# Products of 128 rows in a chunked RWKV-7 recurrence, Gram products of a head pair in one go, and joins of the inverse in another PSUM pool

## The chip, the cores and the metric

The kernel runs on one core of a Trainium2 chip. The metric is device time in microseconds, the median of several runs; one further execution is recorded by the hardware profiler. A core has TensorE (PE, with its weight loads PEld), VectorE (DVE), ScalarE (ACT), GpSimd (POOL) and SyncE (SP, which issues DMAs). They run side by side, each in its own order of instructions, and wait for one another through semaphores.

## The reference

A model of 1024 tokens of width 1024 has two blocks of layers. The first mixes an RWKV-7 recurrence in both directions with MLA attention and is followed by a mixture of experts; the second (windowed attention, a gated linear recurrence, two mixtures of experts) isn't touched here. What matters is the recurrence, eight heads of 64:

```python
def step(state, inp):
    r_t, w_t, k_t, v_t, a_t, b_t = inp
    sa = einsum('bhvk,bhk->bhv', state, a_t)
    state = (state * w_t[:, :, None, :] + sa[..., None] * b_t[:, :, None, :]
             + v_t[..., None] * k_t[:, :, None, :])
    return state, einsum('bhvk,bhk->bhv', state, r_t)

zf = token_shift_centred(z, mu_prev, mu_next)      # r, k, v, wd, ad, gd
a = sigmoid(a0 + einsum('bsdr,drc->bsdc', ad, a_up))   # and decay from tanh(wd) @ w_up
y = wkv7_scan(forward) + flip(wkv7_scan(backward))
```

## The kernel before

A scheduler fixes each engine's order when the program is built; tiles come from pools with a set number of buffers, and an instruction waits until its operands are there and its buffer is free. From 37 to 629 us PE computes the projections z (lines 286 to 288: three fp32r products of high and low parts). Between them stand the preparations of the recurrence. From 631 to 1248 us attention follows: L818, L845, L856 and L873 build keys, values and queries, then come the scores S, the transposes of the probabilities (L900) and the products with the values (L914, L922). After the last finishes of the recurrence the output projection of both branches (br) starts, and from about 1340 us on nothing belongs to the change.

The recurrence works by chunks of 64 tokens: 16 chunks, two directions, four pairs of heads p. The heads of a pair lie on rows 0 to 63 and 64 to 127.

- `prep` runs for each pair, direction d and half of the tokens g (eight chunks). The lora (L580) takes two products of 512 columns, each from 64 rows of a tile. `gram` (L552) multiplies B and K, which stand block-diagonally in tiles bd of 128x128, with AR: the masked results are LT (L557), LA (L559), MB and MK. `flip` transposes (L530) and copies (L532). `put` writes all to rw in DRAM, which holds nine blocks of 128 columns for each two chunks.
- `inverse` inverts the unit triangular matrices of a pair: 32x32 blocks by substitution on DVE (L655, L657), then the two joins of each half of the tokens by products (L679, L683) in PSUM tiles pw.
- `rwkv_chain` carries the state through the 16 chunks of one pair, both directions u at once. Each step loads its blocks (rwt), and `mm` (L742) issues products of 64x64, one per head, direction and summand, that add up in PSUM: px from `ahead` (LA·VT and AN·XT, copied at L761), U = XT·px0 + px1·S (copied at L779), the next state S = KT·VT + BT·U plus the decayed SW (L775, L788), and Y = S·R + VT·MK + U·MB (L792).
- `finish` (L693 to L719) normalises the results of a pair.

Chain 0 starts at 431 us, between the projections; chain 3 ends at 1247 us. PSUM tiles pw (two buffers) belong to the preparations, pc (two buffers) to the chain.

Of the kernel before, what the change touches and what calls it, by code (L numbers as in the profile page):

```python
# [12 lines left out]
OP = mybir.AluOpType  # L13
# [181 lines left out]
class Prog:  # L195
# [22 lines left out]
    def keep(self, keep, dram):  # L218
# [7 lines left out]
        self.rw = [dram.tile([8, 128, 2, 1152], F32, name=f"rw{p}") for p in range(4)]  # L226
# [216 lines left out]

class Rwkv:
# [14 lines left out]
    def own(self, dram, pool, psw):  # L459
# [5 lines left out]
        self.L = [dram.tile([4, 128, NH, CH], F32, name=f"rL{i}") for i in range(2)]  # L465
        self.E = [dram.tile([128, 2, 32, 32], F32, name=f"rE{i}") for i in range(2)]
        for b in range(5):
# [9 lines left out]
    def t(self, name, tag="t"):  # L477
        n = {"t": 9, "l": 2}[tag]
        return (self.big if tag == "t" else self.pp).tile([128, HT], F32, name=name, tag=tag, bufs=n)
# [9 lines left out]
    def put(self, p, d, g, m, t):  # L489
        self.P.nc.sync.dma_start(self.P.rw[p][4 * g:4 * g + 4, :, d, 128 * m:128 * m + 128].rearrange("g p t -> p g t"),  # L490
                                 t.rearrange("p (g c) t -> p g (c t)", c=2))
# [34 lines left out]
    def flip(self, p, d, g, m, x):  # L526

        P, nc, ps = self.P, self.P.nc, self.ps(0)
        for q in range(4):
            nc.tensor.transpose(ps[:, 128 * q:128 * q + 128], x[:, 128 * q:128 * q + 128], P.c("ident"))  # L530
        t = self.t("flip")
        nc.scalar.activation(t, ps, AF.Copy)  # L532
        for c in range(2):
            o = 128 * m + 64 * c
            nc.sync.dma_start(P.rw[p][4 * g:4 * g + 4, :, d, o:o + 64].rearrange("g (h t) k -> t (g h) k", h=2),
                              t[64 * c:64 * c + 64].rearrange("t (x k) -> t x k", k=64))

    def diag(self, i, f):

        t = self.bd[i]  # L540
        for h in range(2):
            s = slice(64 * h, 64 * h + 64)
            f(t[s, :, s], s)
        return t

    def gram(self, lb, AR, da, mask, dr):

        P, nc = self.P, self.P.nc
        for g in range(2):
            ps = self.ps(0)  # L550
            for c in range(4):
                nc.tensor.matmul(ps[:, 128 * c:128 * c + 128], lb[:, 4 * g + c], AR[:, :, 4 * g + c], start=True, stop=True)  # L552
            v = ps.rearrange("p (c x t) -> p c x t", x=2, t=CH)
            cs = slice(4 * g, 4 * g + 4)
            m = lambda name: P.c(name)[:, None, :].to_broadcast([128, 4, CH])
            if mask is None:
                nc.scalar.activation(da[:, cs], v[:, :, 0], AF.Copy)  # L557
            else:
                nc.vector.tensor_mul(da[:, cs], v[:, :, 0], m(mask))  # L559
            nc.vector.tensor_mul(dr[:, cs], v[:, :, 1], m("m_inc"))  # L560

    def prep(self, p, d, g):
# [16 lines left out]
        for x, act in enumerate((P.twd, P.ad)):  # L579
            nc.tensor.matmul(pm[x], up[rows[x], x], act[rows[x], ts], start=True, stop=True)  # L580
# [26 lines left out]
        self.put(p, d, g, 1, AR[:, 1])  # L607
        ta3, kd3, iW3 = c3(ta), c3(kd), c3(iW)
        B = self.diag(0, lambda o, s: nc.vector.tensor_mul(o, ta3[s], iW3[s]))
        K = self.diag(1, lambda o, s: nc.vector.tensor_mul(o, kd3[s], iW3[s]))  # L610
# [9 lines left out]
        LT, MB = self.t3("rLT", "l"), self.t3("rMB")  # L620
        self.gram(B, AR, LT, None, MB)
        self.put(p, d, g, 3, MB)
        self.flip(p, d, g, 0, AR[:, 0].rearrange("p c t -> p (c t)"))
        self.flip(p, d, g, 5, ta)
        LA, MK = self.t3("rLA"), self.t3("rMK")
# [1420 lines left out]
```

## Time and profile before

| | |
|---|---|
| median of 3 runs | 4181.69 us (4176.91 to 4192.26) |
| the profiled execution | 4153.57 us |
| its span; granted clock of PE | 4151.8 us; 0.948 |
| PE busy in the span | 3737.5 us (90%) |
| DVE, ACT, POOL busy | 2816.6 (68%), 2112.2 (51%), 417.2 us (10%) |

Busy time of PE is modelled and overlaps from one matmul to the next; the distance of two starts tells what a matmul takes of PE's time. An f32 matmul leaves two records. The granted clock is a share of full speed: 1.0 is 2.4 GHz and 0.5 is 1.2 GHz, and a value between is a mean over time at either.

### The profile page before, as it was taken

What the parts mean: (1) busy time and instruction counts of PE and PEld (TensorE: products, weight loads), DVE (VectorE), ACT (ScalarE), POOL (GpSimd) and SP (SyncE); (2) the same over time, 40 slices, a digit from 0 to 9 for tenths busy, and PEclk for the clock granted to TensorE, in tenths of its full rate; (3) what the DMA queues carried; (4) which work ended last, traced back from release to release, by engine and by line L of the source; (5) the groups of instructions that cost most, each with busy time, mean ns of one, the idle gap of its engine ahead of it and who ended that gap; (6) DMA issues with size and microseconds to landing.
All of it is one profiled execution on the core that took longest, in us unless ns stands there. A gap on an engine that the chain in (4) does not pass through costs nothing. (4 is left out here: it accounts for less than half of the span.)

```text
span 4151.8 us, 57961 instructions
## 1 busy us (share of the span) xinstructions
PE 3737.5 (90%) x22538; PEld 2975.9 (72%) x22538; DVE 2816.6 (68%) x4374; ACT 2112.2 (51%) x2621; POOL 417.2 (10%) x313
## 2 busy tenths in 40 slices
PE   7999998999997979996999869999969986999994
PEld 6877776777675766664889757887748875788873
DVE  5556374958756556654366778888867766788887
ACT  4322323443332335554255546777738753677774
POOL 0000000100000014330000011111010000111101
PEclk9999998999998989998999989999979997999997
DMA  3355757563437569984233569999731355999994
GB/s 109 130 165 148 215 166 212 148 191 116 161 109 261 183 241 319 315 272 139 112 97 97 217 261 344 384 383 380 284 127 71 114 191 216 333 379 375 383 372 159
DMA packets 371044, 921.87 MB, mean 222 GB/s; under 512 B 156304, under 2 KB 214416, under 8 KB 298832
## 3 DMA queue, kind: packets, MB, share of 16 engines
q1 hardware_dynamic: 352336, 867.78, 57.9%
q0 software_dynamic: 18432, 50.36, 4.8%
q8 instruction: 178, 2.92, 0.3%
q14 instruction: 98, 0.80, 0.1%
HBM read 767.54 MB, written 167.25 MB: 225 GB/s over the span
## 5 line engine op out<-in xcount | busy, mean ns | idle before, releaser
L255 DVE TENSOR_TENSOR wlo<-wraw,whi 128x2048 fp32r<-128x2048 f32 x498 | 1134.1, 2289 | 297.9 <-ACT whi L255 295.3
L255 ACT ACTIVATE whi<-wraw 128x2048 fp32r<-128x2048 f32 x498 | 955.1, 1919 | 366.8 <-PE g L288 243.0
L287 PE MATMUL g<-wlo,xth 128*128 128x512 f32 x1280 | 509.2, 398 | 5.7 <-DVE wlo L255 5.6
L286 PE MATMUL g<-whi,xth 128*128 128x512 f32 x1280 | 511.4, 400 | 3.2 <-ACT xth L255 2.4
L288 PE MATMUL g<-whi,xtl 128*128 128x512 f32 x1280 | 506.8, 396 | 5.9 <-DVE xtl L255 5.6
L288 PEld LDWEIGHTS g<-whi,xtl 128*128 128x128 f32 x1280 | 242.6, 190 | 62.0 <-DVE xtl L255 10.6
L287 PEld LDWEIGHTS g<-wlo,xth 128*128 128x128 f32 x1280 | 243.1, 190 | 59.4 <-DVE wlo L255 7.9
L286 PEld LDWEIGHTS g<-whi,xth 128*128 128x128 f32 x1280 | 243.2, 190 | 57.3 <-ACT xth L255 4.8
L286 PE MATMUL z<-hT_hi,w_hi 128*128 128x512 f32 x592 | 240.8, 407 | 8.0 <-DVE z_out L402 6.4
L1646 POOL DMA_INDIRECT e_xg<-xm,e_ix x32 | 75.5, 2359 | 1711.2 <-DVE e_ix L1644 952.3
L287 PE MATMUL z<-hT_lo,w_hi 128*128 128x512 f32 x592 | 239.5, 404 | 0.0
L288 PE MATMUL z<-hT_hi,w_lo 128*128 128x512 f32 x592 | 238.3, 403 | 0.0
L287 PE MATMUL g<-wlo,e_hh 128*128 128x512 f32 x512 | 202.4, 398 | 15.2 <-DVE wlo L255 15.2
L286 PE MATMUL g<-whi,e_hh 128*128 128x512 f32 x512 | 204.4, 400 | 8.2 <-ACT e_hh L255 8.0
L288 PE MATMUL g<-whi,e_hl 128*128 128x512 f32 x512 | 196.5, 391 | 0.2
L775 POOL TENSOR_SCALAR SW<-S,wc 128x64 f32<-128x64 f32 x120 | 67.2, 575 | 773.6 <-DVE S L788 440.3
L286 PEld LDWEIGHTS z<-hT_hi,w_hi 128*128 128x128 f32 x592 | 113.3, 191 | 38.5 <-DVE z_out L402 6.6
L288 PEld LDWEIGHTS z<-hT_hi,w_lo 128*128 128x128 f32 x592 | 112.8, 191 | 31.6 <-issue 6.1
L287 PEld LDWEIGHTS z<-hT_lo,w_hi 128*128 128x128 f32 x592 | 113.5, 192 | 27.5 <-issue 2.3
L1246 PE MATMUL g<-wraw,m_hT 128*128 128x512 f32 x256 | 117.3, 598 | 13.6 <-ACT m_y L1247 6.8
L287 PEld LDWEIGHTS g<-wlo,e_hh 128*128 128x128 f32 x512 | 96.4, 188 | 42.9 <-DVE wlo L255 24.9
L286 PEld LDWEIGHTS g<-whi,e_hh 128*128 128x128 f32 x512 | 96.3, 188 | 32.9 <-ACT e_hh L255 14.4
(522 smaller groups left out, 8040.9 us busy)
## 6 DMA issues: line engine op xcount, KB each, us to landing
wraw<-in_w_gu SPq DMA_DIRECT2D x256, 1024.0 KB
wraw<-in_w_dn SPq DMA_DIRECT2D x128, 1024.0 KB
wraw<-in_w SPq DMA_DIRECT2D x96, 1024.0 KB
rwt<-rw SPq DMA_DIRECT2D x32, 1152.0 KB
w_raw<-in_w_in SPq DMA_DIRECT2D x37, 512.0 KB
rw<-flip SPq DMA_DIRECT2D x128, 128.0 KB
gt<-z_out SPq DMA_DIRECT2D x16, 512.0 KB
gate<-gt SPq DMA_DIRECT2D x32, 256.0 KB
```

The source lines that it names most:

```text
L255: return self.nc.scalar.activation(hi, src, AF.Copy), self.nc.vector.tensor_sub(lo, src, hi.bitcast(F32))
L286: t.matmul(ps, lh, rh, start=first, stop=False)
L287: t.matmul(ps, lh, rl, start=False, stop=False)
L288: t.matmul(ps, ll, rh, start=False, stop=last)
L775: nc.gpsimd.tensor_scalar(SW[:, d], S[:, d], P.wc[:, c, 4 * d + p:4 * d + p + 1], None, op0=OP.mult)
L1246: nc.tensor.matmul(ps, ht[:, k], w[:, k, n], start=(k == 0), stop=(k == 1))
L1646: nc.gpsimd.indirect_dma_start(out=xg, out_offset=None, in_=self.x, in_offset=bass.IndirectOffsetOnAxis(ap=ix[:, :1], axis=0))
```

## The change

In the chain the operands of two summands that are added lie one above the other on 128 rows, so that one product of 128 rows and 64 columns takes the place of two products of 64 rows. For this the state S and px share a tile SP (S of a head on its own half of the rows, px on the other), U is written into the loaded tile beside V, and rw has a new layout (one chunk, 768 columns). U, S and px are therefore copied half by half. In the preparations B and K of a head stand side by side in KB on that head's 64 rows, and `gram` multiplies them for both heads, by halves of the rows, in two PSUM tiles at once. The lora is split into quarters of 128 columns that alternate between the two tiles. The joins of the inverse take a PSUM tile pc instead of pw. The loads rwt go by two DMAs for each chunk and have three buffers instead of two.

```diff
+VU1, XX0, AN, RR, LL, W3, W2, VU0, XX1, RW = 0, 64, 128, 192, 256, 384, 512, 640, 704, 768
+VU, XX = (VU0, VU1), (XX0, XX1)
+HALF = (slice(0, 64), slice(64, 128))
...
+    def pairs(self, p, d, g, half, o, t):
+        w = t.shape[2]
         for c in range(2):
+            self.P.nc.sync.dma_start(self.P.rw[p][NH * g + c:NH * g + NH:2, HALF[half], d, o:o + w]
+                                     .rearrange("q t k -> t q k"), t[HALF[c]])
...
+    def gram(self, p, d, g, KB, AR):
         P, nc = self.P, self.P.nc
+        m = lambda name: P.c(name)[:, None, :].to_broadcast([128, 4, CH])
+        for q in range(2):
+            pm = [self.ps(0) for h in range(2)]
             for c in range(4):
+                for h in range(2):
+                    nc.tensor.matmul(pm[h][:, 128 * c:128 * c + 128],
+                                     KB[HALF[h], 4 * q + c].rearrange("p x t -> p (x t)"),
+                                     AR[HALF[h], :, 4 * q + c], start=True, stop=True)
+            lw = self.pp.tile([128, 4, 4, CH], F32, name="rLW", bufs=2)
+            for h in range(2):
+                v = pm[h].rearrange("p (c x t) -> p c x t", x=2, t=CH)
+                nc.vector.tensor_mul(lw[:, :, h], v[:, :, 0], m("m_str"))
+                nc.vector.tensor_mul(lw[:, :, 2 + h], v[:, :, 1], m("m_inc"))
+            self.put(p, d, NH * g + 4 * q, slice(0, 128), LL, lw.rearrange("p c x t -> p c (x t)"))
...
-        for x, act in enumerate((P.twd, P.ad)):
-            nc.tensor.matmul(pm[x], up[rows[x], x], act[rows[x], ts], start=True, stop=True)
+        for q in range(4):
+            for x, act in enumerate((P.twd, P.ad)):
+                o = ts.start + 128 * q
+                nc.tensor.matmul(pm[x][:, 128 * q:128 * q + 128], up[rows[x], x], act[rows[x], o:o + 128],
+                                 start=True, stop=True)
...
+            nc.vector.tensor_mul(KB[s, :, h], kd3[s], iW3[s])
+            nc.vector.tensor_mul(KB[s, :, 1 - h], ta3[s], iW3[s])
...
+        tt = [t4(self.t("flip")) for x in range(2)]
+        for x, y in enumerate((kd, ta)):
+            ps = self.flip(y)
+            for h in range(2):
+                copy(tt[h ^ x][:, :, h], ps[:, :, h])
+        for h in range(2):
+            self.pairs(p, d, g, h, W2, tt[h].rearrange("p q h k -> p q (h k)"))
+        t = t4(self.t("flip"))
+        copy(t, self.flip(v))
+        for h in range(2):
+            self.pairs(p, d, g, h, VU[h], t[:, :, h])
...
-            ps = self.ps(0).rearrange("p (x c t) -> p x c t", x=2, t=32)
+            ps = self.ps().rearrange("p (x c t) -> p x c t", x=2, t=32)
...
-                self.put(p, d, g, 8, self.inv[2 * g + d])
+                for h in range(2):
+                    self.put(p, d, NH * g, HALF[1 - h], XX[h], self.inv[2 * g + d][HALF[h]])
...
+        for l, r, half, o in terms:
+            i = nc.tensor.matmul(ps[HALF[half], o:o + 64], l, r, start=last[half] is None, stop=True,
+                                 skip_group_check=True)
+            if last[half] is not None:
+                P.order(i, last[half])
+            last[half] = i
...
+    def part(c):
+        R = pool.tile([128, 2, RW], F32, name="rwt", bufs=3)
+        for h, o in enumerate((AN, 0)):
+            nc.sync.dma_start(R[HALF[h], :, o:o + RW - AN], P.rw[p][c][HALF[h], :, o:o + RW - AN])
...
+        t = [(la[h][HALF[h], u], vu[h][HALF[h], u], 1 - h, 64 * u) for u in U2 for h in range(2)]
+        if c:
+            t += [(an[HALF[1 - h], u], xx[h][HALF[1 - h], u], h, 128 + 64 * u) for u in U2 for h in range(2)]
+        mm(ps, t)
+        for h in range(2):
+            nc.scalar.activation(SP[HALF[1 - h], :, h], v(ps)[HALF[1 - h]], AF.Copy)
+            if c:
+                nc.scalar.activation(xx[h][HALF[h]], v(ps, 128)[HALF[h]], AF.Copy)
...
+                nc.gpsimd.tensor_mul(SW[s], SP[s, :, h], P.wc[s, c, p:8:4][:, :, None].to_broadcast([64, 2, CH]))
...
+        mm(ps, [(xx[h][both[h], u], SP[both[h], u, h], 1 - h, 64 * u) for u in U2 for h in range(2)])
+        nc.vector.tensor_copy(vu[0][HALF[1]], v(ps)[HALF[1]])
+        nc.vector.tensor_copy(vu[1][HALF[0]], v(ps)[HALF[0]])
...
+            mm(ps, [(w2[h][:, u], vu[h][:, u], h, 64 * u) for u in U2 for h in range(2)])
+            SPn = new()
+            for h in range(2):
+                s = HALF[h]
+                if c:
+                    nc.vector.tensor_add(SPn[s, :, h], v(ps)[s], SW[s])
+                else:
+                    nc.vector.tensor_copy(SPn[s, :, h], v(ps)[s])
...
+        t = [(SP[HALF[h], u, h], rr[HALF[h], u], h, 64 * u) for u in U2 for h in range(2)] if c else []
+        mm(ps, t + [(vu[h][:, u], w3[h][:, u], h, 64 * u) for u in U2 for h in range(2)])
...
```

The rows that follow are PE's order as the two programs fix it: line, operation, out<-in, size, and how many in a row.

PE where attention starts, before: L742 is the chain, L818 and L845 attention, L683 a join, L552 a Gram, L580 the lora.

```order
L818 MATMUL pj<-cst,srs 128x128 x4
L742 MATMUL pc<-px,rwt 64x64 x4
L742 MATMUL pc<-S,px 64x64 x4
L742 MATMUL pc<-rwt,S 64x64 x4
L742 MATMUL pc<-rwt 64x64 x4
L818 MATMUL pj<-cst,srs 128x128 x4
L742 MATMUL pc<-rwt,U 64x64 x4
L742 MATMUL pc<-rwt 64x64 x4
L818 MATMUL pj<-cst,srs 128x128 x4
L742 MATMUL pc<-px,rwt 64x64 x4
L742 MATMUL pc<-rwt 64x64 x4
L845 MATMUL pj<-zk,wk 128x512 x2
```

The same place after (the chain is L759, attention L844, the lora L585, a Gram L555, the transposes L536, joins L700 and L704):

```order
L844 MATMUL pj<-cst,srs 128x128 x4
L585 MATMUL pw<-ad,lora_up 128x128 x4
L759 MATMUL pc<-SP,rwt 64x64 x4
L759 MATMUL pc<-rwt 64x64 x4
L759 MATMUL pc<-rwt,SP 64x64 x4
L759 MATMUL pc<-rwt 64x64 x12
L759 MATMUL pc<-SP,rwt 64x64 x4
L759 MATMUL pc<-rwt 64x64 x4
L759 MATMUL pc<-rwt,SP 64x64 x4
L759 MATMUL pc<-rwt 64x64 x12
L759 MATMUL pc<-SP,rwt 64x64 x4
L759 MATMUL pc<-rwt 64x64 x4
```

The size is that of the result, so products of 64 and of 128 rows read alike. Steps of the chain now follow one another (the shown pattern goes on until the fourth ends), with joins and Grams behind them; before, pieces of attention and of preparations stood between the products of a step.

PE among the projections, before: a Gram is one row of eight matmuls on full tiles.

```order
L287 MATMUL z<-hT_lo,w_hi 128x512
L288 MATMUL z<-hT_hi,w_lo 128x512
L286 MATMUL z<-hT_hi,w_hi 128x512
L552 MATMUL pw<-rAR,bd_199 128x128 x8
L287 MATMUL z<-hT_lo,w_hi 128x512
L288 MATMUL z<-hT_hi,w_lo 128x512
```

After, by the numbers of the tiles: the halves of a Gram write pw_1420 and pw_1421.

```order
L288 MATMUL z_5191<-hT_hi_212,w_lo_5161 128x512
L408 MATMUL z_5219<-cstb_67,z_pad_5157 128x2 x4
L555 MATMUL pw_1420<-rAR_1384,rKB_1392 128x128 x4
L555 MATMUL pw_1421<-rAR_1384,rKB_1392 128x128 x4
L408 MATMUL z_5219<-cstb_67,z_pad_5157 128x2 x4
L286 MATMUL z_5237<-hT_hi_212,w_hi_5233 128x512
```

The two halves stand four and four, each on 64 rows, and other work follows them.

PE at the end of attention, before: L914 and L922 are attention, L742 the chain, L695 and L497 the finishes, br the output projection.

```order
L742 MATMUL pc<-px,rwt 64x64 x4
L742 MATMUL pc<-S,px 64x64 x4
L742 MATMUL pc<-rwt,S 64x64 x4
L742 MATMUL pc<-rwt 64x64 x4
L900 MATMUL pt<-cst,p 128x128 x4
L914 MATMUL po<-pts,V 64x128 x8
L742 MATMUL pc<-rwt,U 64x64 x4
L914 MATMUL po<-pts,V 64x128 x7
L922 MATMUL po<-cst,m 64x128 x2
L695 MATMUL pc<-y_8353,cstb 128x512
L497 MATMUL pc<-cstb,t_8362 128x2 x4
L286 MATMUL br_12610<-oh,whi 128x512
```

After (L926, L940 and L948 are attention's):

```order
L948 MATMUL po<-cst,m 64x128 x2
L926 MATMUL pt<-cst,p 128x128 x4
L940 MATMUL po<-pts,V 64x128
L926 MATMUL pt<-cst,p 128x128 x8
L940 MATMUL po<-pts,V 64x128 x15
L948 MATMUL po<-cst,m 64x128 x2
L286 MATMUL br_12328<-oh,whi 128x512
L287 MATMUL br_12328<-ol,whi 128x512
```

Chain and finishes now stand ahead of these rows, and the output projection follows attention directly.

## Rows read from the trace of the kernel before

**Rows 1.** Windows: busy us of each engine (instructions), then PEclk, DMA share, GB/s.

```profile
37.00:1250.00 1213.00, 1144.25 (x9921) 886.93 (x9920) 746.28 (x1663) 410.42 (x777) 70.58 (x126) 0.96 0.52 155
630.00:712.00 82.00, 65.10 (x671) 48.34 (x670) 44.51 (x87) 27.24 (x58) 7.29 (x12) 0.77 0.76 228
1250.00:1275.00 25.00, 13.48 (x40) 9.56 (x41) 16.06 (x34) 10.12 (x11) 0.00 (x0) 0.59 0.95 350
```

**Rows 2.** Timeline of PE: start us, duration us, instruction, x records, at two places.

```profile
430.51 0.40 PE L286 MATMUL z<-hT_hi,w_hi 128*128 128x512 f32 x1
430.75 0.40 PE L287 MATMUL z<-hT_lo,w_hi 128*128 128x512 f32 x1
431.07 0.45 PE L742 MATMUL pc<-rwt 64*64 64x64 f32 x8
431.45 0.50 PE L288 MATMUL z<-hT_hi,w_lo 128*128 128x512 f32 x1
...
549.04 0.40 PE L288 MATMUL z<-hT_hi,w_lo 128*128 128x512 f32 x1
549.37 0.45 PE L742 MATMUL pc<-px,rwt 64*64 64x64 f32 x8
...
550.22 0.50 PE L286 MATMUL z<-hT_hi,w_hi 128*128 128x512 f32 x1
```

**Rows 3.** Waits of PE, 37 to 1250 us: total us, times, longest us.

```profile
PE pc L742 <- DVE S L788: 5.1, 3, 2.6
PE pc L742 <- ACT px L761: 4.7, 4, 3.3
...
PE pc L742 <- DMA rwt<-rw: 3.4, 1, 3.4
PE pc L742 <- DVE U L779: 3.2, 5, 1.1
```

**Rows 4.** Timeline of PE: products with attention's values, column halves.

```profile
1245.39 1.09 PE L914 MATMUL po<-pts,V 128*64 128x128 f32 x16
1246.41 0.45 PE L742 MATMUL pc<-rwt,U 64*64 64x64 f32 x8
```

**Rows 5.** Timeline of PE: a Gram, full tiles.

```profile
192.31 1.95 PE L552 MATMUL pw<-rAR,bd 128*128 128x128 f32 x16
194.01 0.48 PE L287 MATMUL z<-hT_lo,w_hi 128*128 128x512 f32 x1
```

**Rows 6.** Timeline of PE: the lora, one half alone and both halves.

```profile
216.84 1.12 PE L580 MATMUL pw<-twd,lora_up 64*128 64x512 f32 x2
217.89 0.49 PE L288 MATMUL z<-hT_hi,w_lo 128*128 128x512 f32 x1
...
251.82 0.69 PE L580 MATMUL pw<-twd,lora_up 64*128 64x512 f32 x1
251.83 0.69 PE L580 MATMUL pw<-ad,lora_up 64*128 64x512 f32 x1
...
252.88 0.50 PE L286 MATMUL z<-hT_hi,w_hi 128*128 128x512 f32 x1
```

**Rows 7.** Groups by line, 37 to 1250 us: busy us, mean ns | idle before.

```profile
L761 ACT ACTIVATE px<-pc 128x256 f32<-128x256 f32 (+1 forms) x64 | 24.0, 376 | 69.0 <-PE pc L742 68.9
...
L779 DVE COPY U<-pc 128x128 f32<-128x128 f32 x64 | 18.2, 285 | 37.3 <-PE pc L742 36.9
...
L792 ACT ACTIVATE Y<-pc 128x128 f32<-128x128 f32 x64 | 17.5, 274 | 60.6 <-PE pc L742 60.4
...
L788 DVE TENSOR_TENSOR S<-pc,SW 128x128 f32<-128x128 f32 x56 | 16.0, 285 | 27.3 <-PE pc L742 26.9
```

**Rows 8.** Timeline of PE, then of ACT, at the end of attention.

```profile
1247.61 0.48 PE L922 MATMUL po<-cst,m 128*64 128x128 f32 x3
...
1264.13 0.79 PE L286 MATMUL br<-oh,whi 128*128 128x512 f32 x1 [2.58 <-ACT whi L255]
...
1258.48 0.63 ACT L255 ACTIVATE oh<-oraw 128x512 fp32r<-128x512 f32 x1 [10.07 <-DMA oraw<-om]
```

More of the change, by code (lines that the diff above doesn't have):

```diff
@@ L225, in keep @@
         self.gt = [dram.tile([128, T], F32, name=f"gt{j}") for j in range(16)]
-        self.rw = [dram.tile([8, 128, 2, 1152], F32, name=f"rw{p}") for p in range(4)]
+        self.rw = [dram.tile([NCH, 128, 2, RW], F32, name=f"rw{p}") for p in range(4)]
         self.kn = [dram.tile([128, T], F32, name=f"kn{j}") for j in range(4)]
@@ L464, in own @@
             self.P.nc.gpsimd.memset(t, 0.0)
-        self.L = [dram.tile([4, 128, NH, CH], F32, name=f"rL{i}") for i in range(2)]
         self.E = [dram.tile([128, 2, 32, 32], F32, name=f"rE{i}") for i in range(2)]
-        for b in range(5):
+        for b in range(3):
             t = pool.tile([128, NH, 128], F32, name=f"bd{b}", bufs=1)
@@ L477, in t @@
     def t(self, name, tag="t"):
[L478 to L479 removed]
+        return self.big.tile([128, HT], F32, name=name, tag=tag, bufs=9)
     def t3(self, name, tag="t"):
@@ L551, in gram @@
             for c in range(4):
[L552 to L559, printed above, removed]
@@ L728, in rwkv_chain @@
     U2 = range(2)
-    h2 = [slice(0, 64), slice(64, 128)]
     pst = lambda: psum.tile([128, 512], F32, name="pc", bufs=2)
-    new = lambda name: pool.tile([128, 2, CH], F32, name=name, bufs=2)
-    v = lambda ps: ps[:, 0:128].rearrange("p (u t) -> p u t", t=CH)
+    v = lambda ps, o=0: ps[:, o:o + 128].rearrange("p (u t) -> p u t", t=CH)
     def mm(ps, terms):
         last = [None, None]
-        n = len(terms(0))
-        for x in range(n):
-            for u in U2:
-                l, r, o = terms(u)[x]
-                for h in range(2):
-                    i = nc.tensor.matmul(ps[h2[h], 128 * o + 64 * u:128 * o + 64 * u + 64], l[h2[h]], r[h2[h]],
-                                         start=(x == 0 and u == 0), stop=(x == n - 1), skip_group_check=True)
-                    if last[h] is not None:
-                        P.order(i, last[h])
-                    last[h] = i
@@ L748, in parts @@
-    def parts(c):
-        if c % 2 == 0:
-            parts.R = pool.tile([128, 2, 1152], F32, name="rwt", bufs=2)
-            nc.sync.dma_start(parts.R, P.rw[p][c // 2])
-        o = CH * (c % 2)
-        return [parts.R[:, :, 128 * m + o:128 * m + o + CH] for m in range(9)]
-    def ahead(c, q):
-        AN, _, LA, _, _, _, _, VT, XT = q
-        n = 2 if c else 1
-        ps = pst()
-        mm(ps, lambda u: [(LA[:, u], VT[:, u], 0)] + ([(AN[:, u], XT[:, u], 1)] if c else []))
-        t = pool.tile([128, 2, 2, CH], F32, name="px", bufs=2)
-        nc.scalar.activation(t[:, 0:n], ps[:, 0:128 * n].rearrange("p (x u t) -> p x u t", u=2, t=CH), AF.Copy)
-        return t
@@ L764, in rwkv_chain @@
-    S = None
-    q = parts(0)
-    px = ahead(0, q)
+        for l, r, half, o in terms:
[8 more added lines that the diff above has]
+            nc.sync.dma_start(R[HALF[h], :, o:o + RW - AN], P.rw[p][c][HALF[h], :, o:o + RW - AN])
+        one = lambda m: R[:, :, m:m + CH]
+        two = lambda *m: [one(x) for x in m]
+        return (one(AN), one(RR), two(LL, LL + CH), two(W2, W2 + CH), two(W3, W3 + CH), two(*VU), two(*XX))
@@ L767, in rwkv_chain @@
+    new = lambda: pool.tile([128, 2, 2, CH], F32, name="SP", bufs=3)
+    q, SP = part(0), new()
+    ahead(0, q, SP)
     for c in range(NCH):
-        _, Rr, _, MB, MK, BT, KT, VT, XT = q
+        _, rr, _, w2, w3, vu, xx = q
         if c % 2 == 0:
@@ L795, in rwkv_chain @@
                 nc.sync.dma_start(P.yd[4 * d + p][:, CH * (c - 1):CH * (c + 1)], Y[:, d].rearrange("p c t -> p (c t)"))
-        S = Sn
         if c < NCH - 1:
-            q = parts(c + 1)
-            px = ahead(c + 1, q)
+            q = part(c + 1)
+            ahead(c + 1, q, SPn)
+        SP = SPn
 def mla(P, dram, pool, psum):
```

94 lines of the change are left out of this document (36 added, 58 removed).

## The prediction

> **What bounds the kernel now.** I first read the windows view of the stage that the change touches [rows 1]. From 37 to 1250 us PE is busy 1144.25 of 1213 us at a granted clock of 0.96, DVE 746.28, ACT 410.42, POOL 70.58. So this stage is bound by PE, with two soft places: 630 to 712, where attention starts (65.10 of 82 us, granted clock 0.77), and 1250 to 1275 (13.48 of 25, clock 0.59). After 1340 us both kernels issue the same work, and I count nothing there.
>
> In a stage bound by PE a change is worth the time between starts of PE's instructions, not their modelled durations, which overlap. So I read starts from the timeline. The recurrence's small products stand between projection matmuls that start every 0.24 us (430.51, 430.75). Eight records of L742 (an f32 matmul leaves two) push the next projection matmul from 0.24 to 0.70 us after the last; twenty-four push it to 1.18 [rows 2]. Sixteen records more cost 0.48 us: **29 to 30 ns a record** (I use 29.2). The rest, 0.70 − 0.235 − 8 × 0.0292 = 0.23 us, belongs to the block itself: it goes from full tiles to 64x64 tiles and back, **0.12 us for each change of tile shape**.
>
> Then the waits. In this stage PE waited on the recurrence's U 3.2 us, on its px 4.7, on its state S 5.1, together 12 times [rows 3]. The hand-offs between engines are nearly all hidden by preparations, projections and attention.
>
> **The change part by part.**
>
> *Stacked summands in the chain.* Over four chains the program issues 2224 matmuls of 64x64 before, and after it 1488: 736 fewer. Of those left about half have 128 rows and 64 columns. The question is what such a one costs. Before, the two heads of a pair sit on different rows and columns of the array, and 29.2 ns is the price of two running side by side. The stacked form fills all rows, so its two halves can run side by side only by columns. The trace has that form in L914, 128*64 tiles with twice the moving columns: 16 records in 1245.39 to 1246.41, less the 0.09 that a shape change costs in these starts, 58 ns a record [rows 4]. A full-tile matmul of 128 columns takes 1.70 us for 16 records, 106 ns each [rows 5]. 58 is near half of 106, so column halves do overlap, and 64 columns should cost half of 58, 29 ns. Term: 736 × 2 × 29.2 ns = **−43 us**. Other bound: 0, if with 64 columns the halves don't overlap (then the 736 × 2 records left in stacked form cost twice 29.2 ns, which gives back what the fewer ones save).
>
> *Joint Grams.* Before, 256 matmuls of block-diagonal 128 rows at 2 × 106 ns: 54 us. After, 256 matmuls that use 64 rows each. Row halves overlap fully where one of each half is next to another: in the lora both halves took 251.82 to 252.88, 1.06 us, and one half alone took 216.84 to 217.89, 1.05 us [rows 6]. All paired, that saves 27 us. But in the new order the halves often stand four and four. Walking the new PE order with the two halves overlapped where such runs meet gives −22.7, and with only direct neighbours overlapped −14.6. The second matmul of 251.83 started 0.01 us after the first, so a half need not wait for the other; I take **−20**, bounds −27 and −15.
>
> *Lora in quarters.* The same columns, 128 matmuls of 128 for 32 of 512. In the new order 22 of the 28 blocks hold one half alone, about as before; **0**, bounds ±1.5 (one 1.05 us pairing won or lost).
>
> *Changes of tile shape.* Gram and lora pieces now need row halves, and the scheduler scatters them among projections, attention and chain. Counting neighbours of different tile shape in PE's order up to the last attention matmul: 555 before, 715 after. At 0.12 us, **+19**. By starts of L914 against full tiles (0.09) it would be +15.
>
> By the Trainium skill ("TensorEngine Tiling (Array Packing)", Key Properties) a change of tiling mode drains the engine. The 0.12 us above agrees with that, and the rule speaks against the change; the sum would be the same with it.
>
> By the Trainium skill ("TensorE: Matmul & The Clock Gate", Part 3) matmuls start and end strictly in program order. Grams standing four and four would by it come to −15 in place of −20, and the sum to −34.
>
> *More hand-offs.* Each step now copies U with two DVE copies where one took 285 ns, writes S with two adds where one took 285, and px with four ACT copies (274 ns for 128x128) where one took 376 [rows 7]: 0.285 + 0.285 + 0.72 = 1.29 us more in a step. It costs only where nothing covers it. Before, 5, 4 and 3 of 64 hand-offs were waited for [rows 3]; the same share gives 5 × 0.285 + 4 × 0.72 + 3 × 0.285 = **+5**. Bounds 0 and 64 × 1.29 = 83. DVE gets 64 copies, 60 adds and 32 Gram products more; at even twice 285 ns these 156 are 89 us on an engine with 467 us free in this stage: nothing. What hides it is PE's own work; without that cover the price is the 83 above. The doubled loads queue on SP, and rwt has three buffers instead of two: nothing, with the one wait of 3.4 us on rwt [rows 3] as the bound either way.
>
> *Joins from the chain's PSUM.* Eight joins now take turns with the chain, and preparations no longer wait for them. No such wait shows among [rows 3]; 0.
>
> *End of the stage.* Before, the last finishes follow the last attention matmul (1247.61) and the first output projection starts at 1264.13. After, they all stand ahead of it. But ACT waited 10.07 us for attention's own output to come back from DRAM, until 1258.48 [rows 8]; that remains. Saved: at most 5 us (16.0 less 10.07 and the conversion). Moved forward into a PE-bound stretch: at most the PE work of this place at full clock, 13.48 × 0.59 = 8 us, of which most leaves places that were cold and half idle. **0**, bounds −5 and +8.
>
> **Sum**: −43 − 20 + 0 + 19 + 5 + 0 = −39. The profiled execution lasted 4153.57 us and would become 4115. The median shown is 4181.69, 28 us above the profiled one; I take those 28 as belonging to both, so 4181.7 − 39 = **4143**. About 0.5%, 21 us, is what a measurement of this kernel can tell from no change.
>
> **The rivals.**
>
> *A, the sum (0.56).* Its own range by the bounds: −43 − 27 − 2 + 15 + 0 − 5 = −62 and −43 − 15 + 2 + 19 + 25 (twenty of 64 steps exposed) + 8 = −4: 4120 to 4178.
>
> *B, more than the sum (0.15).* With the joins off the preparations' PSUM and three rwt buffers, attention's start might fill: 82 − 65.10 = 16.9 us idle, and 65.10 × (1 − 0.77/0.96) = 12.9 for the clock. With Grams fully paired (−7 more) that is −76: 4106. Against it: the new order puts four chain steps there with nothing between them.
>
> *C, given back at attention's start (0.12).* Ten steps of the chain stand there with little cover. Each exposes U's copies (0.57) and px's four (1.1), less the 0.23 us of S·R products beside them: some 1.5 us, 15 together with nothing else. If the clock then falls from 0.77 to the 0.59 of [rows 1], the same work takes 65.10 × 0.77 / 0.59, 20 us more. 35 of the 39 are gone: 4178, no change. For it: PE was already at 0.77 there with better cover.
>
> *N, the stacked form brings nothing (0.07).* Column halves with 64 columns don't overlap: −39 + 43 = +4, 4186. Against it: the 58 ns of L914.
>
> *D, slower (0.10).* The chain becomes the bound. Without hand-offs the sum is −44; each exposed step gives 1.29 us back, so from 34 steps of 64 nothing is gained, and from 50 the kernel is slower by over 0.5%; all 64 give +39, 4221. For it: longer hand-offs and 144 more DMAs on SP. Against it: the 12 waits in 64 steps.
>
> **How the numbers follow.** The predicted time is A's. From 4098 to 4190 lie nearly all of A, half of B, C and N: 0.56 + 0.08 + 0.12 + 0.06, eight in ten. Faster by over 0.5% (under 4161) are five sixths of A and all of B, and some of C: 0.66. Within 0.5% are the rest of A, C and N: 0.24. Slower: D, 0.10.
>
> **What the profile of the changed kernel would show.** Start to start, eight records of the stacked product between projection matmuls should again cost 0.70 us; 0.9 or more would be N. A Gram of eight matmuls should take about 0.9 us where sixteen records took 1.70. PE's busy share from 37 us to the first output projection should stay near 94%, with that projection some 35 to 45 us earlier. Waits of the chain on U, px and S should stay under 20 us; 40 or more, gathered after attention's start with the clock under 0.77, is C; spread over all chains it is D. The stage after 1340 should last as long as before. The prediction is wrong if the changes of tile shape cost much more than 0.12 us between small tiles of different kind, which no row of before shows apart, or if the chain runs alone more often than the order's neighbours suggest.

## The result, and the profile after

The change made the kernel slower: 4226.65 us in the median (4223.22 to 4234.24), against 4179.3 before; the ratio is 1.0126 (95% interval 1.0108 to 1.0143), where the two medians alone give 1.0113. The profiled execution after lasted 4229.44 us, near its median; that of before, 4153.57 us, lies under the four that stand beside it, so the two traces differ by 76 us where the timed runs differ by 47 (by 58 against the 4169 us that before gave in the later comparisons). Only the parts of the difference are read from the traces.

The windows view of the kernel after, by stages (projections; to the first scores; attention; to the first output projection), with the columns of [rows 1]:

```profile
38.00:606.00 568.00, 555.26 (x3108) 441.82 (x3108) 326.03 (x739) 172.89 (x313) 12.42 (x24) 0.97 0.53 156
606.00:741.00 135.00, 103.12 (x884) 82.77 (x883) 79.42 (x168) 43.18 (x114) 9.72 (x22) 0.67 0.83 218
741.00:1335.00 594.00, 516.79 (x4686) 380.25 (x4685) 408.47 (x959) 226.39 (x537) 32.12 (x72) 0.93 0.53 139
1335.00:1349.00 14.00, 0.35 (x6) 0.10 (x1) 3.92 (x8) 3.78 (x5) 0.00 (x0) 0.60 0.80 282
```

And the same stages before:

```profile
37.00:628.00 591.00, 567.44 (x3413) 451.79 (x3413) 324.11 (x719) 174.67 (x288) 17.26 (x30) 0.97 0.52 154
628.00:705.00 77.00, 60.62 (x611) 44.94 (x608) 38.31 (x76) 26.98 (x56) 5.23 (x10) 0.76 0.76 227
705.00:1248.00 543.00, 516.10 (x5902) 390.21 (x5900) 382.87 (x865) 208.48 (x432) 48.09 (x86) 0.99 0.49 146
1248.00:1264.00 16.00, 4.01 (x11) 2.28 (x10) 7.41 (x22) 4.29 (x6) 0.00 (x0) 0.61 0.85 310
```

The projections take 23 us less, as they should with fewer matmuls between them. Then 58 us are lost ahead of the scores and 51 in attention; the output stage then gains 14, and the rest to the end is within 5 of before. In both stages PE waits more and the granted clock is lower: 0.67 instead of 0.76, and 0.93 instead of 0.99.

That gives a way to sort the difference. From the first projection product to the last product of the output, busy time of PE times granted clock (by slices of some 5 us) is its **work** at full speed; busy time less work is what the **slow clock** costs; the rest is **idle**. Before: 1313.8 + 42 + 91 = 1447 us. After: 1285.7 + 90 + 142 = 1517. Work fell by 28 us, the slow clock took 48 and idle time 51. By place: of the 58 us ahead of the scores 22 are work that stood elsewhere before, 21 slow clock and 16 idle time. Attention has 26 us less work, and its 51 us more are 26 of slow clock and 50 of idle time.

Three places of the timeline after show the price of the products. All lie among projections, at full clock:

```profile
436.84 0.40 PE L287 MATMUL z<-hT_lo,w_hi 128*128 128x512 f32 x1
437.17 0.69 PE L759 MATMUL pc<-rwt 128*64 128x64 f32 x16
437.78 0.50 PE L288 MATMUL z<-hT_hi,w_lo 128*128 128x512 f32 x1
...
563.62 0.40 PE L286 MATMUL z<-hT_hi,w_hi 128*128 128x512 f32 x1
563.95 0.45 PE L759 MATMUL pc<-rwt 128*64 128x64 f32 x8
564.33 0.45 PE L759 MATMUL pc<-rwt,SP 64*64 64x64 f32 x8
564.71 0.45 PE L759 MATMUL pc<-rwt 128*64 128x64 f32 x8
565.09 0.50 PE L287 MATMUL z<-hT_lo,w_hi 128*128 128x512 f32 x1
...
604.00 1.72 PE L555 MATMUL pw<-rAR,rKB 64*128 64x128 f32 x16
605.65 0.50 PE L287 MATMUL z<-hT_lo,w_hi 128*128 128x512 f32 x1
```

Sixteen stacked records alone push the next z by 0.94 us (436.84 to 437.78). Sixteen 64x64 records with their two changes of shape would by [rows 2] cost 0.235 + 16 × 0.0292 + 0.23, which is 0.93. So a stacked record costs what a 64x64 record costs. The step over 24 records of both kinds takes 1.47 us; less one z and 24 × 0.0292 this leaves 0.53 for four changes of tile shape, 0.13 each: a change between two small shapes costs as much as one from a full tile. A Gram's eight matmuls, four and four, took 1.65 us, hardly less than on full tiles [rows 5].

The waits of PE after, from the first projection to the last attention product:

```profile
PE pt L926 <- DVE m L916: 13.5, 9, 3.6
PE pt L926 <- DVE pts L930: 11.3, 10, 2.9
PE po L940 <- DVE tab L900: 10.1, 4, 8.2
PE pc L759 <- ACT rwt L783: 9.3, 11, 2.1
...
PE pc L759 <- DMA rwt<-rw: 6.3, 3, 2.9
...
PE pc L759 <- DVE rwt L801: 5.6, 11, 1.6
```

The chain's own hand-offs (L783 px, L801 U) are 15 us in 22 waits, little more than the 13 of [rows 3]. The largest waits are attention's, for its own softmax (m, pts: 25 us) and its tables (10). Added up over attention alone, waits that DVE ended are 62 of its 77 us idle, where before they were 24 of 27. In 48 of the 62 DVE was at work, most of all on the softmax (copies to pts 11, maxima 9). Yet its busy share in attention didn't rise: 408 of 594 us after, 383 of 543 before. Ahead of the scores the order puts chain steps one after another:

```profile
621.17 1.88 PE L759 MATMUL pc<-rwt 128*64 128x64 f32 x24
623.80 1.13 PE L759 MATMUL pc<-SP,rwt 128*64 128x64 f32 x8 [0.76 <-ACT rwt L783]
625.32 1.00 PE L759 MATMUL pc<-rwt 128*64 128x64 f32 x8 [0.39 <-DVE rwt L801]
626.26 0.69 PE L759 MATMUL pc<-rwt,SP 64*64 64x64 f32 x8
626.88 1.74 PE L759 MATMUL pc<-rwt 128*64 128x64 f32 x24
629.38 1.13 PE L759 MATMUL pc<-SP,rwt 128*64 128x64 f32 x8 [0.76 <-ACT rwt L783]
```

A step takes 5.58 us (623.80 to 629.38), for 48 records that cost 1.4 us at full speed, changes of shape left out.

### The profile page after: what moved, and what is told of

Its sections match the earlier page's. It is cut to its first block, busy times and chain, and to the rows that moved or that the text cites. A ratio compares the mean times of both kernels' runs of the same rounds, so it can differ in the third digit from the quotient of the medians.

```text
span 4227.6 us, 56040 instructions
## 1 busy us (share of the span) xinstructions
PE 3756.9 (89%) x21258; PEld 2986.9 (71%) x21258; DVE 2868.6 (68%) x4530; ACT 2142.2 (51%) x2805; POOL 394.9 (9%) x303
## 5 line engine op out<-in xcount | busy, mean ns | idle before, releaser
L759 PE MATMUL pc<-rwt 64*64 64x64 f32 (+1 forms) x1984 | 113.9, 244 | 15.8 <-DMA rwt<-rw 6.3
L759 PEld LDWEIGHTS pc<-rwt 64*64 64x64 f32 (+1 forms) x1984 | 86.4, 148 | 55.0 <-issue 21.6
```

What stands on the lines that cost most here:

```text
L759: i = nc.tensor.matmul(ps[HALF[half], o:o + 64], l, r, start=last[half] is None, stop=True, skip_group_check=True)
```

## The experiments

Three theories: **1**, the order that the scheduler draws (steps and preparations piled up ahead of the scores) is the loss; **2**, the products cost more than reckoned; **3**, the hand-offs cost everywhere. A run's ratio is to the kernel before, timed beside it. Stages and parts are those of the section above, in us.

| run | median | ratio (95% interval) | to scores | attention | work | slow clock | idle |
|---|---|---|---|---|---|---|---|
| before | 4166 to 4179 | 1 | 77 | 543 | 1314 | 42 | 91 |
| after | 4226.65 | 1.0126 (1.0108 to 1.0143) | 135 | 594 | 1286 | 90 | 142 |
| e1 | 4224.08 | 1.0138 (1.0119 to 1.0157) | 77 | 593 | 1289 | 84 | 128 |
| e2 | 4172.65 | 1.0012 (1.0001 to 1.0023) | 56 | 617 | 1286 | 66 | 107 |
| e3 | 4186.01 | 1.0044 (1.0030 to 1.0058) | 118 | 573 | 1274 | 86 | 119 |
| e4 | 4188.83 | 1.0050 (1.0033 to 1.0067) | 92 | 588 | 1290 | 72 | 109 |
| e5 | 4165.85 | 0.9998 (0.9988 to 1.0008) | 71 | 565 | 1313 | 52 | 97 |
| e6 | 4174.19 | 1.0016 (1.0006 to 1.0026) | 76 | 545 | 1326 | 42 | 86 |
| e7 | 4233.34 | 1.0158 (1.0141 to 1.0175) | 164 | 559 | 1293 | 82 | 155 |
| e8 | 4322.23 | 1.0377 (1.0357 to 1.0398) | 130 | 555 | 1300 | 105 | 208 |
| e9 | 4214.03 | 1.0097 (1.0079 to 1.0114) | 127 | 585 | 1284 | 98 | 127 |
| e10 | 4171.75 | 1.0004 (0.9995 to 1.0014) | 110 | 561 | 1281 | 74 | 103 |
| e11 | 4227.16 | 1.0127 (1.0106 to 1.0149) | 110 | 618 | 1280 | 90 | 145 |
| e12 | 4154.57 | 0.9963 (0.9949 to 0.9977) | 98 | 543 | 1281 | 59 | 104 |
| e13 | 4224.48 | 1.0134 (1.0112 to 1.0155) | 116 | 599 | 1285 | 97 | 131 |
| e14 | 4208.01 | 1.0097 (1.0075 to 1.0118) | 129 | 557 | 1287 | 89 | 119 |
| e15 | 4159.23 | 0.9980 (0.9967 to 0.9994) | 70 | 586 | 1280 | 63 | 111 |
| e16 | 4166.34 | 0.9995 (0.9986 to 1.0005) | 130 | 511 | 1312 | 49 | 96 |
| e17 | 4202.39 | 1.0086 (1.0069 to 1.0103) | 115 | 594 | 1279 | 82 | 136 |
| e18 | 4245.06 | 1.0195 (1.0178 to 1.0212) | 69 | 580 | 1297 | 101 | 133 |

Work is good to about 10 us: three kernels with the old products (before, e5, e16) agree within 2, a fourth (e6) stands 13 above.

**Single edits of the changed kernel, e1 to e4.** In turn: joins on the old pool, two load buffers, Gram halves in strict turn, the lora whole.

```diff
-            ps = self.ps().rearrange("p (x c t) -> p x c t", x=2, t=32)     # e1
+            ps = self.ps(0).rearrange("p (x c t) -> p x c t", x=2, t=32)
-        R = pool.tile([128, 2, RW], F32, name="rwt", bufs=3)                # e2
+        R = pool.tile([128, 2, RW], F32, name="rwt", bufs=2)
+                    if last is not None: P.order(i, last)                   # e3, in gram
-        for q in range(4):                                                  # e4
-            for x, act in enumerate((P.twd, P.ad)): ...
+        for x, act in enumerate((P.twd, P.ad)):
+            nc.tensor.matmul(pm[x], up[rows[x], x], act[rows[x], ts], start=True, stop=True)
```

> The changed kernel with the joins of the inverse on the preparations' PSUM again (one word). All products, copies and loads stay as changed, only the order and the two pools differ. In PE's order 152 matmuls of the chain and 56 of preparations and joins stand between the last projection matmul and the first scores, where the changed kernel has 280 and 152. Theory 1 (the order: chain and preparations piled up ahead of the scores, exposed and on a slow clock, are the loss): from the last projection to the first scores some 75 to 90 us instead of 135, and the kernel about 4180. Theory 2 (the stacked and half-row products cost more than reckoned): about 4225 as the changed kernel. Theory 3 (the hand-offs cost everywhere): 4215 to 4230.

The stretch ahead of the scores fell to 77 us as theory 1 said, and the total did not follow: chain 3 ended at 1320 us instead of 1262, and the stretch from the first output projection to its last product grew from 207 to 255. By the total alone theories 2 and 3 had it right.

> The changed kernel with two buffers for the chain's loads instead of three. 124 matmuls of the chain and 56 of preparations stand ahead of the scores. Theory 1 (the order): 70 to 85 us from the last projection to the first scores, about 4175 to 4185. Theory 2 (products): about 4225. Theory 3 (hand-offs, loads): 4225 or more, since a buffer less can only add waits for the loads.

54 us faster than the changed kernel with one buffer less and the same instructions: against theories 2 and 3. PE even waited longer for the loads (16.1 us in attention). The stretch ahead of the scores is shorter than theory 1 said (56 us against 70 to 85), and attention longer by 23.

> The changed kernel with the two halves of each Gram forced to alternate matmul by matmul. 228 matmuls of the chain and 152 of preparations stand ahead of the scores. Theory 1 (the order): 110 to 130 us there, about 4205 to 4215. By the products alone: eight Gram matmuls should take some 0.9 to 1.1 us among projections everywhere, where four and four took 1.65 at 604.00 us in the changed kernel; if the halves overlap only as neighbours that is up to 8 us less in all, otherwise nothing. Theory 2: up to 8 us off the changed kernel, no more.

Faster than its theory's number. The Grams, from the timeline (fourteen of sixteen records stand between two projections):

```profile
192.11 1.16 PE L556 MATMUL pw<-rAR,rKB 64*128 64x128 f32 x14
193.20 0.50 PE L288 MATMUL z<-hT_hi,w_lo 128*128 128x512 f32 x1
```

1.09 us for fourteen in turn, 1.65 for sixteen four and four: halves overlap as neighbours only. Over the kernels with all the new products and the copies as changed, the work is 1287 us on average in the seven without turns (after, e1, e2, e4, e9, e13, e14: 1284 to 1290) and 1279 in the six with turns (e3, e10, e11, e12, e15, e17: 1274 to 1281). A record takes 78 ns in turns and 103 four and four, by these starts; halves that overlap in full would take 53, half of the 106 of [rows 5].

> The changed kernel with the lora in two products of 512 columns again. 192 matmuls of the chain and 84 of preparations stand ahead of the scores. Theory 1 (the order): 85 to 105 us there, about 4185 to 4200. Theory 2 (products): within 5 us of the changed kernel. Theory 3 (hand-offs): the same as the changed kernel.

As theory 1 said, at its lower end.

**Parts put into the old kernel, e5 to e8.** e5 is e1's edit the other way round in the kernel before. e6 splits the copies:

```diff
-        nc.vector.tensor_copy(Ut, v(ps))
+        for h in h2: nc.vector.tensor_copy(Ut[h], v(ps)[h])
-                nc.vector.tensor_add(Sn, v(ps), SW)
+                for h in h2: nc.vector.tensor_add(Sn[h], v(ps)[h], SW[h])
-        nc.scalar.activation(t[:, 0:n], ps[:, 0:128 * n] ..., AF.Copy)
+        for x in range(n):
+            for h in h2: nc.scalar.activation(t[h, x], v(ps[:, 128 * x:])[h], AF.Copy)
```

e7 has the changed chain with `gram`, `diag` and the lora of before; e8 the changed `gram`, KB and lora with the chain, the layout and the joins of before. Only the `put`s and a few buffers are adapted.

> The kernel before with one word changed: the joins of the inverse take the chain's PSUM. No instruction is added or removed. In its order 224 matmuls of the chain and 68 of preparations and joins stand ahead of the first scores (before 208 and 72). If the joins' pool is the cause of the loss: 4200 or more, with longer waits of the chain. If the loss lies in the order that the scheduler draws for the new chain, and that draw is a matter of chance: within 15 us of before either way, by PE's idle time and clock alone. If the loss lies in the new copies or products: 4165 to 4175, as before.

No difference: the joins' pool isn't the cause.

> The kernel before with the copies of U, the additions to S and the copies of px split into halves of the rows, as the changed kernel has them (1.29 us more of DVE and ACT in each of the 64 steps, some 83 us in all); products, loads and layout stay as before. Theory 3 (hand-offs): slower by 20 to 60 us, with more waits of PE on U, S and px and on the softmax behind them on DVE. Theory 1 (only the order) : within 15 us of before, since 256 matmuls of the chain and 76 of preparations stand ahead of the scores, little more than before. Theory 2 (products): no change at all.

Theory 3 falls in the old chain: 6 us, by the interval 3 to 11, where 20 to 60 were expected. The groups by line of this run, for U and px:

```profile
L763 ACT ACTIVATE px<-pc 64x128 f32<-64x128 f32 x248 | 67.2, 271 | 80.3 <-PE pc L742 75.6
...
L782 DVE COPY U<-pc 64x128 f32<-64x128 f32 x128 | 36.6, 286 | 27.3 <-PE pc L742 24.8
```

A copy of 64 rows takes as long as one of 128 [rows 7], so DVE carries 34 us more (U and S) and ACT 43, and the old chain hides them.

> The chain of the changed kernel with the Gram and the lora of before (the Gram results are written to the new layout by eight DMAs for each preparation). 400 matmuls of the chain and 160 of preparations stand ahead of the scores, more than in the changed kernel. Theory 1 (order): the stretch from the last projection to the scores 135 us or more, total 4220 or more; busy time times clock of PE some 20 to 40 us under before. Theory 2 (products): that sum not under before. Theory 3 (hand-offs): waits on U, px and S spread over all four chains.

With the chain alone the whole loss is there, with 21 us less work. It is one order of this chain, and it has 128 small writes of Gram results where the changed kernel has 32.

> The Gram and the lora of the changed kernel with the chain, the layout and the joins of before (16 DMAs write the Gram results for each preparation). 480 matmuls of the old chain, which are 13 steps, and 120 of preparations stand ahead of the scores. Theory 1 (order): that stretch 110 us or more where before has 77, total 4190 to 4220, though the chain is the old one. Theory 2 (products of the chain) and theory 3 (hand-offs of the chain): 4160 to 4180, since neither is in it.

This one doesn't tell what it should. Its Gram results go out by 28 small writes for each preparation (not the 16 of the expectation), on the queue that loads the projections' weights: ACT waited 60.1 us for w_raw, and the projections alone took 697 us with PE idle for 80. Behind the projections it does tell something, though: with the old chain it lost nearly as much there as e7 with the new one (the table by place below).

**The order alone, e9 to e15.** A rule is a dependence in PE's order, without a change to any instruction:

```diff
+        P.steps[p, c] = mm(ps, ...)                       # first product of a step
+        for k in HOLD.get(P.scores, ()): P.order(P.steps[k], i)   # behind score number P.scores
+HOLD = {0: [(1, 1)]}          # e9, e10 (with turns), e13, e15; in e11: {c: [(1, c + 1)] for c in range(15)}
+LATER = {0: [(2, 1, 0)]}      # e13, e14: the lora of that preparation; in e15: (2, 0, 1)
```

> The changed kernel with one rule of order added: the second step of chain 1 may not stand ahead of the first scores in PE's order. Every instruction, tile and pool is that of the changed kernel. 132 matmuls of the chain and 168 of preparations and joins now stand ahead of the scores, where the changed kernel has 280 and 152. If the order is the cause: that stretch 85 to 110 us instead of 135, total 4185 to 4205. If products or hand-offs are: 4220 to 4230.

> The same rule of order with the halves of a Gram forced to alternate. 128 matmuls of the chain and 148 of preparations ahead of the scores. If the order and the pairing of halves add up: 4170 to 4190, and busy time times clock of PE some 10 us under the run without alternation. If not: as the run with the rule alone.

> Alternating Grams, and a rule for all of chain 1: its step c + 1 may not stand ahead of score c, so that the steps lie spread over the attention. If what remains of the loss is bare waiting of attention for its own softmax, with nothing between, it falls here: idle time of PE from the first scores to the last attention product 35 to 50 us instead of 60 to 77, total 4155 to 4175. If attention waits for other reasons (its loads, DVE): as the run with the rule for one step.

> The changed kernel with two buffers for the chain's loads and alternating Grams, without a rule of order. 132 matmuls of the chain and 112 of preparations ahead of the scores. If the gains of the two single runs (54 us and some 40 us under the changed kernel) came from the same place, the order, they don't add: 4160 to 4185. If they were separate costs they add: about 4130 to 4140.

The rule alone won 12 us, and the stretch it was meant for only 8; neither reading of e9 came true. With turns it won 55, as e10's first reading said, but work fell by 3 us only from e9 to e10 and not by 10. Spreading the steps (e11) made attention longer, not shorter, against its expectation. e12, with two buffers and turns, beats both kernels: 0.9963, between its two readings. It needs no rule. Its stages:

```profile
599.00:696.00 97.00, 72.34 (x515) 54.86 (x514) 63.91 (x125) 31.79 (x77) 5.72 (x10) 0.68 0.81 215
696.00:1239.00 543.00, 500.73 (x5005) 371.78 (x5005) 408.78 (x964) 233.28 (x566) 38.15 (x84) 0.98 0.61 157
```

Attention at 0.98 of the clock, with 42 us idle instead of 77.

> The changed kernel with two rules of order and nothing else: step 2 of chain 1 (as in the run with the order alone) and the eleventh preparation may not stand ahead of the first scores. Ahead of them: 132 matmuls of the chain, 88 of preparations and joins. If preparations at the start of attention are what is exposed (they pace themselves by their own hand-offs): that stretch 75 to 95 us where one rule gave 127; total 4165 to 4190. If the chain's steps alone were: about 125 us, as with the one rule. If the loss is only moved, since preparations and scores then meet later: the stretch falls, attention grows by as much, total 4205 to 4215.

> The changed kernel with the rule on the eleventh preparation alone: 324 matmuls of the chain and 88 of preparations and joins ahead of the scores. If preparations are what is exposed there: 100 to 115 us, less than the 127 of the rule on the chain, total under 4214. If the chain's steps are: 140 us or more, total 4225 to 4240.

> Two buffers for the loads, alternating Grams, and rules that keep step 2 of chain 1 and the tenth preparation behind the first scores: 112 matmuls of the chain and 64 of preparations ahead of them. If what stands ahead of the scores sets the loss: that stretch 55 to 75 us where the run without rules has 98, total 4115 to 4140. If the loss moves into attention: 4150 to 4165, and PE's idle time in attention 15 us or more above its 42.

The square of four (after, e9, e14, e13) has 135, 127, 129 and 116 us ahead of the scores, and totals of 4227, 4214, 4208 and 4224. The rules together took most from that stretch (e13: 19 us) and won nothing; e14 took 6 there, and its attention is 37 us shorter. So the length of that stretch doesn't set the total, and the numbers of e13 and e14 fit neither reading in full. In e13 attention itself isn't ready: at 685 us PE waits 16.8 us for one copy of ACT. e15 came out as its second reading said: the stretch is 70 us, and attention's idle time 56 instead of e12's 42 (14 more, where the reading named 15).

**The old chain in the new order, e16.** The first key product of attention is held behind the seventh step of chain 1 and the tenth preparation, in the kernel before:

```diff
+AHEAD = [(1, 6), (2, 0, 1)]
+                for f in AHEAD if not (pr or q or k) else (): P.order(i, P.steps[f])
```

> The kernel before, all its instructions, with one rule of order: the first key product of attention may not stand ahead of the seventh step of chain 1 and the tenth preparation. In PE's order 448 matmuls of the old chain (12.4 steps; the changed kernel has 11.7 there) and 140 of preparations and joins then stand ahead of the scores, as in the changed kernel. If the order is what loses the time there, whichever chain it is: 120 to 150 us from the last projection to the scores, total 4205 to 4240. If the new chain, its copies or its loads are needed for the loss: 4165 to 4185.

```profile
626.00:755.00 129.00, 97.61 (x1185) 77.21 (x1186) 69.86 (x159) 41.16 (x89) 15.52 (x24) 0.78 0.79 225
755.00:1266.00 511.00, 487.37 (x5354) 366.18 (x5349) 362.88 (x825) 199.08 (x404) 41.93 (x72) 0.98 0.46 143
```

Theory 1 falls in this form. The stretch grew to 130 us as expected, and attention shrank by 32: steps done early are steps that attention doesn't have to carry, and the total stayed where it was. In the four orders of the old chain with the old products the total hardly changed (before, e5, e6, e16).

> Two buffers, alternating Grams and the whole lora of before, no rule of order: 188 matmuls of the chain and 116 of preparations ahead of the scores. The products save the same; if the total follows the idle time that the order gives, it lies between 4150 and 4190 and not at the 4130 that the saving alone would give.

Two buffers, turns and the whole lora won 54, 41 and 38 us singly, and together 24, 12 us above the range that was expected: these are draws of the order, not costs that add.

**Copies side by side, e18.** Of the changed kernel's copies ACT takes one of U's, and DVE two of px's:

```diff
-        nc.vector.tensor_copy(vu[1][HALF[0]], v(ps)[HALF[0]])
+        nc.scalar.activation(vu[1][HALF[0]], v(ps)[HALF[0]], AF.Copy)
-                nc.scalar.activation(xx[h][HALF[h]], v(ps, 128)[HALF[h]], AF.Copy)
+                nc.vector.tensor_copy(xx[h][HALF[h]], v(ps, 128)[HALF[h]])
```

> The changed kernel with the copies of a hand-off shared between the two engines: of U's two copies ACT takes one, and of the four copies of px DVE takes two. Products, loads, buffers and pools are the changed kernel's; DVE has 56 copies more and ACT 56 fewer. A hand-off is then about half as long. In PE's order 96 matmuls of the chain and 60 of preparations stand ahead of the scores. If the length of the new chain's hand-offs, one copy behind another on one engine, is what the attention stage pays for: 4150 to 4180, waits of PE on the chain's copies under 8 us (15 in the changed kernel) and idle time of PE in attention under 50 us. If it isn't, the run falls among the other draws of the order, 4170 to 4230, and idle time in attention stays at 55 to 75 us.

```profile
PE pc L759 <- DVE rwt L783: 21.7, 23, 5.1
PE pc L759 <- DVE rwt L801: 14.9, 14, 3.8
...
886.02 0.48 PE L759 MATMUL pc<-SP,rwt 128*64 128x64 f32 x2 [5.13 <-DVE rwt L783]
```

The opposite came: waits of the chain on its copies rose from 15 to 37 us, chain 3 ended at 1349 us, and the run is the slowest but e8. Idle time in attention is 60 us, as the second reading said, and the total lies above its range. A copy on DVE takes some 290 ns, but the waits for it reach 5.1 us: it stands in DVE's order behind other work. In the longest, which ended at 886.0 us, DVE worked from 880.5 to 885.7 on an inverse, a preparation and a softmax before the copy's turn came.

**The same parts by place.** In us: work, then slow clock and idle time together, ahead of the scores and in attention.

| run | ahead: work | ahead: clock and idle | attention: work | attention: clock and idle |
|---|---|---|---|---|
| before | 48 | 29 | 510 | 33 |
| after | 70 | 66 | 484 | 110 |
| e2 | 39 | 17 | 506 | 111 |
| e6, old chain | 55 | 21 | 506 | 40 |
| e7, new chain alone | 92 | 72 | 455 | 103 |
| e8, new Grams alone | 70 | 61 | 465 | 89 |
| e12 | 50 | 48 | 494 | 49 |
| e16, old chain piled up | 79 | 50 | 481 | 31 |

Three things stand in it. Piling up does cost clock and idle time ahead of the scores, with the old chain too (50 us against 29), and nearly all that e2 wins over the changed kernel is won there (17 against 66). What the changed kernel loses in attention, e16 doesn't lose. And the loss isn't bound to the new chain: e8 has the old chain, layout and joins, and from the projections to the end of attention it loses 150 us where before loses 62 and e7 175. Its extra writes may have a part in that; of its 66 us idle in attention DMAs ended 2 and DVE 53. Its windows for the two places:

```profile
735.00:866.00 131.00, 88.71 (x1223) 72.73 (x1222) 56.16 (x120) 31.70 (x68) 14.49 (x26) 0.77 0.66 183
866.00:1420.00 554.00, 487.93 (x5089) 369.91 (x5089) 362.83 (x818) 192.38 (x388) 32.99 (x66) 0.94 0.41 122
```

## Why the prediction was wrong

**Stacked products.** The price was right: 29 ns a record (436.84 to 437.78 us), and 736 fewer matmuls. Rival N is out. What they saved in all isn't measured apart; e7, with the new chain alone, has 21 us less work.

**Grams.** −20 was taken, with −15 as the bound for halves that overlap as neighbours only. They do: a Gram took 1.65 us and not the 0.9 that was to be seen, and turns gave 8 us of work, the size of −23 less −15. By the Trainium skill ("TensorE: Matmul & The Clock Gate", Part 3) matmuls start and end strictly in program order; the 1.65 and 1.09 us agree with it.

**Changes of tile shape.** 0.13 us measured between small shapes, 0.12 reckoned. The products and the changes together were to give −44; the work fell by 26 to 28, some 5 of the difference being the Grams, and about 10 the resolution of the figure.

**Joins and lora.** By work nothing, as said: 1289 us in e1 and 1290 in e4, 1286 in the changed kernel. That e4's 38 us come from the order is argued, not shown.

**Hand-offs, and what covers them: the step that failed.** The only term for waiting in the sum was +5, and DVE's 156 more instructions were put at nothing because DVE had 467 us free. Behind both stood the premise that in a stage bound by PE saved work is saved time: I carried the cover of the old order over to a new one. The waits that the +5 names did stay small, 15 us for the chain's copies and 21 with the loads, where 13 and 16 were before. The time went where the sum had no term: idle time of PE rose by 51 us and the slow clock by 48. Most of the idle time came in attention, where PE waited for DVE 62 us instead of 24, above all for attention's own softmax, and the granted clock was 0.93 instead of 0.99. So PE is busy 87% of attention, not 95, and saved work there is no longer saved time: the first output projection starts at 1349 us, 85 later, where 35 to 45 earlier was forecast. DVE's free time was no guard: its busy share in attention is 69%, before 71.

**The rivals.** C named the place and the clock, with 15 us exposed and 20 for the clock, and 16 and 21 were measured there. But of the 32 us idle in that stretch only 11 are waits on the chain's copies; C has nothing for attention, which lost 77 more; and e16 has a like pile-up with no change of the total. D's 4221 lies near the 4226.65 by luck: it stands on 83 us of bare hand-offs, and the waits on them rose by 2 to 3. B's fuller start of attention didn't come: the clock there fell from 0.76 to 0.67.

What is shown: the loss is idle time and slow clock from the end of the projections on, and its size depends on the order. With the new products the kernel takes from 4154.6 us (e12) to 4227.2 (e11) with all copies on the engines of the change, and 4245.1 with some moved (e18). Three variants of the kernel with the old products (e5, e6, e16) lie between 4165.9 and 4174.2. The new chain alone has the loss (e7), but e8 has much of it with the old chain, so which part of the change makes the order worse isn't shown. What stays open is why attention waits so much more in these orders. e18 points at DVE's queue, on which the new chain hands over twice as often; e6, which does the same in the old chain with about as much DVE work in attention (405 us), is against that as the whole reason. The stacking of U, which makes one product wait for both px and S, is a candidate that wasn't tried apart.

## What to carry to other kernels

A saving on the busiest engine is a saving only if the new order still covers the waits of everything else; sort the difference into work, clock and idle time before looking for a cause. Where a scheduler draws the order, run a few neutral edits of both kernels: here another pool moved the new kernel by nothing, a buffer less by 1.3%, and with turns of the Grams by 1.7%, from slower than before to faster. A stretch that grows is no loss until the stretch behind it has been looked at, and its work has been taken out.

## What the runs showed of the hardware that was not expected

Row halves of TensorE overlap only if their matmuls are neighbours in the order: 1.09 us for fourteen records in turn, 1.65 for sixteen four and four. A change between 128x64 and 64x64 tiles costs as much as one from a full tile, 0.13 us. A copy of 64 rows takes 286 ns on DVE and one of 128 rows 285, so splitting by rows doubles the time. PE's waits on DVE in attention rose from 24 to 62 us while DVE's busy share there went from 71% to 69%.
